# A tile's place in memory, late loads and later transposes in a two-layer decoder trunk

## The chip, the cores and the metric

The kernel runs on one core of a Trainium2 chip. The metric is the device time of one execution in microseconds (us). Three runs of the kernel before took 938.87, 939.19 and 939.3 us; the median is 939.19 us. The engines are named as in the profile: PE multiplies matrices (PEld is its loading of the stationary operand), DVE and ACT work on tiles element by element, POOL does small things and issues some DMAs, SP issues the other DMAs.

## The reference

A trunk of two layers on x of 256 x 1024 in float32. Every layer is FFN, attention, FFN. The first attention is stick-breaking, the second a sliding window with sinks that reads keys and values (kv_w) computed from the stream after layer one.

```
def rms_norm(x, g):
    y = xf * lax.rsqrt(jnp.mean(xf * xf, axis=-1, keepdims=True) + RMS_EPS)
    return (y * g)

def swiglu(x, w_in, w_out):
    gate, up = jnp.split(x @ w_in, 2, axis=-1)
    return (jax.nn.silu(gate) * up) @ w_out

for layer in range(DEPTH):                        # DEPTH = 2, D_FF = 2816
    h = h + 0.5 * swiglu(rms_norm(h, ffn1_norm[layer]), ffn1_w_in[layer], ffn1_w_out[layer])
    hn = rms_norm(h, mix_norm[layer])
    if layer < N_A_LAYERS:                        # 16 heads of 64
        qkv = (hn @ sb_w_qkv[layer])
        h = h + stick_breaking_attention(q, k, v) @ sb_w_o[layer]
    else:                                         # 4 kv heads, window 128
        q = rotary(hn @ swa_w_q[j])
        h = h + sliding_window_sink_attention(q, k_shared, v_shared, swa_sinks[j]) @ swa_w_o[j]
    h = h + 0.5 * swiglu(rms_norm(h, ffn2_norm[layer]), ffn2_w_in[layer], ffn2_w_out[layer])
    if layer == N_A_LAYERS - 1:
        kv = rms_norm(h, kv_norm) @ kv_w
        k_shared, v_shared = rotary(k), v
return rms_norm(h, final_norm)
```

## The kernel before, in words

**Products in parts.** Every float32 factor is split in a high part (a cast to float32r) and a low part (the rest). `step` (L226 is the matmul helper `mm` that it calls) makes three matmuls of it: high stationary on high weights, low stationary on high weights, high stationary on low weights. A weight block arrives as `raw`; ACT casts it to `w_hi` (L345) and DVE subtracts to get `w_lo` (L347), in two pieces each. The stationary operand holds 128 rows of the stream, transposed: `xT` after a norm, `aT_h`/`aT_l` after the FFN's gating, `S_h`/`S_l` for sums of quarters of x, `o_h`/`o_l` after an attention, `xkv_h`/`xkv_l` for the shared keys and values. The weight part streams past it, 512 columns at a time. In the queries of the sliding window the weight part is 256 columns wide; in those and the keys of the stick-breaking attention xT moves and the weights are stationary.

**xT** is one tile `[128, 8, 2, 256]` of 16 KB in each partition, which holds both parts. It is requested at the head of the program, ahead of all other tiles, and a tile takes its place in memory when it is requested: in this build byte 8,320 of each partition. Most other tiles (raw, weight parts, aT, S) come from `Slots` and are requested when the first instruction that uses them is written out.

**An FFN** goes over the 2816 columns in six blocks: one plain, one narrow (256 columns), four by Strassen's scheme with seven products of 12 matmuls instead of eight, three of the seven with xT. In each block gate and up are multiplied together (`mul`, L523, or `mul_less`, L652, on DVE), the result m is transposed on PE (`turn`, L532) into the bank `tr` and split into aT_h (ACT) and aT_l (DVE). The output products of a block follow inside the next one. The first FFN's plain block runs while the first weights are still arriving.

**The order.** Every operation is a `Task` with an engine, a duration that the planner assumes, a priority and its dependences. `Plan.order` plays the tasks through and writes them out in the order found. That order is kept on PE, ACT, DVE and POOL (`manual_schedule` names these four). SP is not among them: its DMAs are ordered by the scheduler of the language, from the program as written out. `lat` of a task is the delay that the planner assumes between its end and the start of a task that needs it.

**Norm weights** (`gain`) are loaded by a DMA that spreads 1024 values over 128 partitions, through two slots. The gain of the next norm is requested ahead of the stage at whose end it is used. The sinks and the rotation table `rp` are requested ahead of the first FFN and used in the second half of the program.

Of the kernel before, what the change touches and what calls it, by code (L numbers as in the profile page):

```python
# [17 lines left out]
P = 128  # L18
# [22 lines left out]
BY_DMA = False  # L41
DMA3 = True
FSUMS = 5000.0
WARM = 14
HEAD = 700.0

# [120 lines left out]
def kernel(  # L167
# [34 lines left out]
    RAW, WP, A4 = Slots("raw", RAWS, 8), Slots("w", 2 * PAIRS, 8), Slots("a", 4, 4)  # L202
    STG, S8, G4 = Slots("stg", 6, 3), Slots("s", 2, 8), Slots("g", 2, 4)

    xx = pool.tile([P, KD, 2, S], F32R, name="xT")
    xh, xl = [Buf(lambda i=i: xx[:, :, i]) for i in range(2)]
    hN = fixed([P, NT, D], F32, "hN")
    kT_s, v_s = fixed([P, KVH, S], F32, "kT_s"), fixed([P, NT, KVH * HD], F32, "v_s")
    ps_all = psum.tile([P, 8, 512], F32, name="ps")
# [94 lines left out]
    MWIN = [(consts, f"mw{i}") for i in range(3)] + K0  # L304


    def dma(src, dst, nbytes, w, prio, name=None):
        T("SP", nbytes / (300.0 if prio < -8e5 else PLAIN), lambda: nc.sync.dma_start(out=dst(), in_=src), w=w, prio=prio)

    def gain(vec):  # L310
        g = G4.get([P, D], F32, "gain")
        dma(vec.unsqueeze(0).to_broadcast([P, D]), lambda: g.ap, P * D * 4, B(g), plan.pos + 20000)
        return g


# [153 lines left out]
    def ffn(w_in, w_out, acc, rest, finish, kv=None, blocks=BLOCKS, first=False, ending=False):  # L469
# [50 lines left out]
            T("ACT", act(n), lambda: ACT.activation(out=dst(), in_=src(), func=AF.Silu), r=r + [(consts, "tbl")], w=w)  # L520

        def mul(dst, a_, b_, r, w, n=512):
            T("DVE", dve(n), lambda: DVE.tensor_mul(out=dst(), in0=a_(), in1=b_()), r=r, w=w)  # L523


        def turn(m, t, aT, nk=4):
# [90 lines left out]
        def strassen(n, c, between):  # L617
            a, d, b = ring
            ring[:] = [d, b, a]
            aT = new_a()  # L620
            r11, r12, r22, r21 = [load([(slice(0, 512), col(h, i, c))], 4, 512) for h, i in ((0, 0), (1, 0), (1, 1), (0, 1))]

            def add(dst, src):
                m = 2048 // PIECES
                for i in range(PIECES):
                    sl = slice(m * i, m * i + m)
                    ks = [i] if PIECES == 2 else [0, 1]
                    T("DVE", dve(m), lambda sl=sl: DVE.tensor_add(out=flat(dst)[:, sl], in0=flat(dst)[:, sl], in1=flat(src)[:, sl]),  # L628
                      r=[(src, k) for k in ks], w=[(dst, k) for k in ks], prio=plan.pos - LEAD)
# [12 lines left out]

            def stage(src, name):
                s = STG.get([P, 512], F32, name)
                T("ACT", act(512), lambda: ACT.copy(out=s.ap, in_=src.ap), r=B(src), w=B(s))
                return s

            def plus(s, bank):
                T("DVE", dve(512), lambda: DVE.tensor_add(out=s.ap, in0=s.ap, in1=bank.ap), r=B(bank), w=B(s))

            def mul_less(dst, a_, b_, r, w):
                T("DVE", dve(512), lambda: DVE.scalar_tensor_tensor(out=dst(), in0=b_(), scalar=-1.0, in1=a_(), op0=ALU.mult, op1=ALU.mult),  # L652
                  r=r, w=w)
# [38 lines left out]
            STG.put(p5)  # L692
            turn(m, 1, aT)
            return aT, 4
# [77 lines left out]
    def stick_breaking(w_qkv, w_o, p0, others_, finish):  # L772
# [85 lines left out]
        for t in range(NT):  # L858
            for j in range(2):
                values(j, t)  # L860
        for g in range(4):
            ws = [weight([(slice(0, 256), wv[:, :, s * D + 256 * g:s * D + 256 * g + 256])], KD, 256) for s in range(2)]

            for b in range(2):
                for s in range(2):
                    ps = bank_()
                    for k in range(KD):
                        hi, lo = ws[s]

                        def run(k=k, hi=hi, lo=lo, ps=ps, b=b):  # L870
                            mm(ps.ap, hi.ap[:, k, ts(b)], xx[:, k].rearrange("p a b -> p (a b)"), k == 0, False)
# [33 lines left out]
    def shared_kv(gk, pairs, rstds):  # L905
        kh, kl = WP.get([P, KD, S], F32R, "xkv_h"), WP.get([P, KD, S], F32R, "xkv_l")

        def operands(tr):
            for t in range(NT):
                normed(t, rstds[t], gk, [tr, tr], kh, kl)  # L910

        def run(ring, tr):
            at_ = plan.pos
            plan.pos -= 8000.0
            operands(tr)
            plan.pos = at_
            wv = by_k(kv_w)
            bs = [ring[0], ring[1]]
# [23 lines left out]
    def sliding_window(w_q, w_o, p0, others_, finish):  # L942
# [165 lines left out]
    A4.put(grow)  # L1108

    def finisher(scale, gs, then=None):  # L1110
        g = gain(gs)

        def fin(t, pair):
            add_residual(t, pair, scale)
            normed(t, None, g, pair, xh, xl)
            if t == 1:
                G4.put(g)
        return fin

    rstds = {}  # L1120
# [10 lines left out]
            normed(t, rstds[t], g0, ring_pair((A0, A1)[t]), xh, xl, (j,))  # L1131
    plan.pos = 0.0
    T("POOL", 10, lambda: None, w=B(g0, banks[6], banks[7]))
    for dst, src, n in ((sinks, swa_sinks[0].unsqueeze(0).to_broadcast([P, H]), P * H * 4),
                        (rp, rope.rearrange("(t p) c d -> p t c d", p=P), P * NT * 4 * HD * 4)):
        dma(src, lambda dst=dst: dst.ap, n, B(dst), 40000)
    T("DVE", 150, lambda: DVE.tensor_scalar(out=nsinks.ap, in0=sinks.ap, scalar1=-1.0, scalar2=None, op0=ALU.mult),
      r=B(sinks), w=B(nsinks), prio=60000)

    ffn(ffn1_w_in[0], ffn1_w_out[0], (A0, A1), A2 + A3, finisher(0.5, mix_norm[0]), first=True)  # L1140
    stick_breaking(sb_w_qkv[0], sb_w_o[0], A0, (A1, A2, A3), finisher(1.0, ffn2_norm[0]))
    ffn(ffn2_w_in[0], ffn2_w_out[0], (A0, A1), A2 + A3, finisher(0.5, ffn1_norm[1]))
    gk = gain(kv_norm)
    ffn(ffn1_w_in[1], ffn1_w_out[1], (A0, A1), A2 + A3, finisher(0.5, mix_norm[1]), kv=shared_kv(gk, (A0, A1), rstds))
    sliding_window(swa_w_q[0], swa_w_o[0], A0, (A2, A3, A1), finisher(1.0, ffn2_norm[1]))

    g_fin = gain(final_norm)

    def last(t, pair):
        add_residual(t, pair, 0.5)  # L1150
        hg = [STG.get([P, 512], F32, "hg") for _ in range(2)]
        rstd = root(t)
        for j in range(2):
            T("DVE", dve(512), lambda j=j: DVE.tensor_mul(out=hg[j].ap, in0=hN.ap[:, t, half(j)], in1=g_fin.ap[:, half(j)]),
              r=[(hN, (t, j))] + B(g_fin), w=B(hg[j]), prio=plan.pos + 10)
# [51 lines left out]
```

## Time and profile before

| | |
|---|---|
| median of 3 runs | 939.19 us |
| the profiled execution | 940.11 us, its span 938.3 us |
| PE busy | 926.3 us (99%) |
| DVE busy | 780.7 us (83%) |
| ACT busy | 602.4 us (64%) |
| read from memory | 204.22 MB, 219 GB/s over the span |
| mean granted TensorE clock | 0.997 |

The span runs from the first to the last instruction. A row of a group shows the line, engine and operation, the tiles written and read, the shape and count, then the busy time of the group in us and the mean duration of one in ns, then the idle time of the engine ahead of it. Matmuls follow each other before the one ahead has ended, and their ends are modelled; the distance from start to start is what one costs in a row of them. In a timeline the first number is the start, the second the time that the merged instructions cover.

### The profile page before, as it was taken

The page shows a single profiled execution, that of the slowest core. Times are in us where ns is not written, and L with a number is a line of the kernel's source. Part 1 is how long each engine was busy: PE and PEld are TensorE (multiplying, and loading weights), DVE is VectorE, ACT ScalarE, POOL GpSimd, SP SyncE. Part 2 cuts the span into 40 slices and gives each one's busy share as a digit, 9 for nine tenths or more (in the row PEclk, how much of TensorE's full clock was granted, in tenths as well). Part 3 has the DMA queues.
Part 4 walks back from the last instruction along what each step waited for, and adds up shares of the span by engine and source line. Part 5 has one row for each costly group of instructions (what it writes and reads, how often), then busy time and mean ns, then how long its engine had stood idle before and what let it go on. Part 6 is the DMA issues. An engine that isn't in the chain of part 4 may idle for free.

```text
span 938.3 us, 11890 instructions
## 1 busy us (share of the span) xinstructions
PE 926.3 (99%) x4520; PEld 754.1 (80%) x4520; DVE 780.7 (83%) x929; ACT 602.4 (64%) x851; POOL 51.7 (6%) x62
## 2 busy tenths in 40 slices
PE   9999999999999999999999999999999999999997
PEld 6788888888887888888888888888887788888885
DVE  7879998766666987999879689998798598799983
ACT  6566767556777656766656467676756475676662
POOL 1010101000000000110000001010000000011000
PEclk9999999999999999999999999999999999999999
DMA  9968999866334677999975579999752348699961
GB/s 326 356 154 236 292 279 241 280 202 224 100 126 134 202 201 203 227 311 272 287 250 190 179 184 268 300 283 243 247 191 91 90 143 244 195 231 308 275 174 45
DMA packets 100203, 206.04 MB, mean 220 GB/s; under 512 B 3761, under 2 KB 24497, under 8 KB 100146
## 3 DMA queue, kind: packets, MB, share of 16 engines
q1 hardware_dynamic: 83104, 171.46, 52.0%
q0 software_dynamic: 16896, 33.56, 21.4%
q8 instruction: 35, 0.57, 0.2%
q10 hardware_dynamic: 146, 0.27, 0.1%
q14 instruction: 22, 0.18, 0.1%
HBM read 204.22 MB, written 1.05 MB: 219 GB/s over the span
## 4 chain that ended last, share of the span: by engine, by line
PE 89%; DVE 4%; DMA 4%; issue 1%; ACT 1%; SPq 0%; POOL 0%; POOLq 0%; DVEq 0%; ACTq 0%
PE ps L226 85%; DMA raw<-in_ffn_w_in_dram 3%; PE ps L532 2%; DVE w_lo L347 2%; PE ps L396 1%; DMA raw<-in_swa_w_q_dram 1%; ACT w_hi L345 1%; DVE e L1048 0%; DVE xs L450 0%; ACT sq L421 0%; DVE small L1022 0%; DVE xT L403 0%; DVE hN L463 0%; DVE s L498 0%; PE ps L1055 0%
## 5 line engine op out<-in xcount | busy, mean ns | idle before, releaser
L347 DVE TENSOR_TENSOR w_lo<-raw,w_hi 128x1024 fp32r<-128x1024 f32 x412 | 484.7, 1219 | 46.0 <-ACT w_hi L345 44.2
L345 ACT CAST w_hi<-raw 128x1024 fp32r<-128x1024 f32 x412 | 410.6, 1049 | 122.0 <-PE ps L226 58.3
L226 PE MATMUL ps<-w_hi,xT 128*128 128x512 f32 (+1 forms) x960 | 288.8, 384 | 0.9 <-ACT xT L402 0.6
L226 PEld LDWEIGHTS ps<-w_hi,xT 128*128 128x128 f32 x960 | 175.2, 189 | 37.4 <-ACT xT L402 0.9
L226 PE MATMUL ps<-w_lo,xT 128*128 128x512 f32 (+1 forms) x480 | 183.0, 381 | 0.0
L226 PE MATMUL ps<-w_hi,aT_h 128*128 128x512 f32 x352 | 139.3, 396 | 0.0
L226 PE MATMUL ps<-w_lo,aT_h 128*128 128x512 f32 x352 | 137.5, 391 | 0.0
L226 PE MATMUL ps<-w_hi,aT_l 128*128 128x512 f32 x352 | 137.0, 389 | 0.0
L226 PEld LDWEIGHTS ps<-w_lo,xT 128*128 128x128 f32 x480 | 90.6, 189 | 18.9
L226 PE MATMUL ps<-w_hi,S_h 128*128 128x512 f32 x256 | 101.6, 397 | 0.0
L226 PE MATMUL ps<-w_lo,S_h 128*128 128x512 f32 x256 | 100.1, 391 | 0.0
L226 PE MATMUL ps<-w_hi,S_l 128*128 128x512 f32 x256 | 99.7, 389 | 0.0
L226 PEld LDWEIGHTS ps<-w_lo,aT_h 128*128 128x128 f32 x352 | 66.1, 188 | 14.2
L226 PEld LDWEIGHTS ps<-w_hi,aT_l 128*128 128x128 f32 x352 | 66.2, 188 | 13.3
L226 PEld LDWEIGHTS ps<-w_hi,aT_h 128*128 128x128 f32 x352 | 66.1, 188 | 13.0
L628 DVE TENSOR_TENSOR raw<-raw 128x1024 f32<-128x1024 f32 x64 | 76.1, 1219 | 0.4
L633 POOL DMA_DIRECT2D raw<-in_ffn_w_in_dram x32 | 41.0, 1282 | 537.7 <-ACT w_hi L345 224.5
L226 PEld LDWEIGHTS ps<-w_lo,S_h 128*128 128x128 f32 x256 | 48.0, 188 | 10.4
L226 PEld LDWEIGHTS ps<-w_hi,S_l 128*128 128x128 f32 x256 | 48.1, 188 | 9.7
L226 PEld LDWEIGHTS ps<-w_hi,S_h 128*128 128x128 f32 x256 | 48.1, 188 | 9.7
L402 ACT CAST aT_h<-ps 128x512 fp32r<-128x512 f32 (+1 forms) x48 | 26.4, 550 | 35.2 <-PE ps L532 35.1
L226 PE MATMUL ps<-xT,w_hi 128*128 128x512 f32 x128 | 46.5, 401 | 0.0
(154 smaller groups left out, 889.5 us busy)
## 6 DMA issues: line engine op xcount, KB each, us to landing
raw<-in_ffn_w_in_dram SPq DMA_DIRECT2D x76, 1024.0 KB, 7.8
raw<-in_ffn_w_out_dram SPq DMA_DIRECT2D x44, 1024.0 KB, 5.2
raw<-in_ffn_w_in_dram POOLq DMA_DIRECT2D x32, 1024.0 KB, 9.3
raw<-in_sb_w_qkv_dram SPq DMA_DIRECT2D x12, 1024.0 KB, 6.6
raw<-in_ffn_w_in_dram SPq DMA_DIRECT2D x16, 512.0 KB, 5.0
raw<-in_ffn_w_in_dram SPq DMA_DIRECT2D x16, 256.0 KB, 5.4
raw<-in_sb_w_o_dram SPq DMA_DIRECT2D x4, 1024.0 KB, 5.1
raw<-in_swa_w_q_dram SPq DMA_DIRECT2D x4, 1024.0 KB, 9.4
```

What stands on the lines that cost most here:

```text
L226: PE.matmul(ps, lhsT=lhsT, rhs=rhs, start=start, stop=stop, skip_group_check=True)
L345: T("ACT", act(m), lambda sl=sl: ACT.copy(out=flat(hi)[:, sl], in_=flat(raw)[:, sl]), r=[(raw, i) for i in rs] + first, w=[(hi, i) for i i ...
L347: T("DVE", dve(m), lambda sl=sl: DVE.tensor_sub(out=flat(lo)[:, sl], in0=flat(raw)[:, sl], in1=flat(hi)[:, sl].bitcast(F32)), r=[(raw, i) ...
L396: PE.transpose(out=bank.ap[:, i * P:(i + 1) * P], in_=s, identity=ident)
L402: T("ACT", act(n), lambda: ACT.copy(out=hi[2](), in_=src()), r=B(bank), w=[hi[0:2]])
L532: PE.transpose(out=tr.ap[:, i * P:(i + 1) * P], in_=m.ap[:, i * P:(i + 1) * P], identity=ident)
L628: T("DVE", dve(m), lambda sl=sl: DVE.tensor_add(out=flat(dst)[:, sl], in0=flat(dst)[:, sl], in1=flat(src)[:, sl]), r=[(src, k) for k in ks ...
L633: T("POOL", 1500, lambda: nc.gpsimd.dma_start(out=dst.ap, in_=src, accum_op=ALU.add), w=[(dst, 0), (dst, 1)], prio=plan.pos - LOADS, lat=5 ...
```

## The change

Four edits, as the diff below shows them:

- xT is requested when the first instruction that writes it is written out, behind the first raw tiles and weight parts. In the build its place goes from byte 8,320 to byte 85,600 of each partition. The tiles that lay between the two, two of the weight slots, two of the raw slots and one of the two aT_l slots among them, move down by 16,384 bytes; the rest stay, but for a swap of an aT_h and a gain slot.
- Each gain is requested at the end of its stage, with a dependence on a marked late tile of that stage and an earlier priority than the point of request; the sinks and `rp` are requested behind the stick-breaking attention, with a dependence of the same kind. The dependence is the planner's; no data goes over it.
- `mul` and `mul_less` get a `lat` of 1180 instead of 180: the planner counts with 1000 ns more until the transposes of their result may run.
- `nsinks`, one small DVE operation on the sinks, moves with them.

```
+TM = 1000.0
...
-    xx = pool.tile([P, KD, 2, S], F32R, name="xT")
-    xh, xl = [Buf(lambda i=i: xx[:, :, i]) for i in range(2)]
+    xT = Buf(lambda: pool.tile([P, KD, 2, S], F32R, name="xT"))
+    xh, xl = [Buf(lambda i=i: xT.ap[:, :, i]) for i in range(2)]
...
-    def dma(src, dst, nbytes, w, prio, name=None):
+    def dma(src, dst, nbytes, w, prio, r=()):
...
+    marks = []
     def gain(vec):
         g = G4.get([P, D], F32, "gain")
-        dma(vec.unsqueeze(0).to_broadcast([P, D]), lambda: g.ap, P * D * 4, B(g), plan.pos + 20000)
+        dma(vec.unsqueeze(0).to_broadcast([P, D]), lambda: g.ap, P * D * 4, B(g), plan.pos - 25000, marks)
...
-            T("DVE", dve(n), lambda: DVE.tensor_mul(out=dst(), in0=a_(), in1=b_()), r=r, w=w)
+            T("DVE", dve(n), lambda: DVE.tensor_mul(out=dst(), in0=a_(), in1=b_()), r=r, w=w, lat=LAT["DVE"] + TM)
...
-                  r=r, w=w)
+                  r=r, w=w, lat=LAT["DVE"] + TM)
...
+            if n == last - 1:
+                marks[:] = [(outs[n][0][0], 1)]
...
+        marks[:] = [(v, (0, 1))]
...
+        marks[:] = [(qT, (2, 1))]
...
     def finisher(scale, gs, then=None):
-        g = gain(gs)
+        g = []
         def fin(t, pair):
+            if t == 0:
+                g.append(gain(gs))
             add_residual(t, pair, scale)
-            normed(t, None, g, pair, xh, xl)
+            normed(t, None, g[0], pair, xh, xl)
...
-        dma(src, lambda dst=dst: dst.ap, n, B(dst), 40000)
+        dma(src, lambda dst=dst: dst.ap, n, B(dst), plan.pos - 60000, marks)
```

What becomes of it in the order of the instructions is shown at three places. The first is PE's queue where the first FFN's plain block ends (its last products with xT) and the transposes of its first m stand. Before:

```order
L226 MATMUL ps<-w_hi,xT 128x512 x2
L226 MATMUL ps<-w_lo,xT 128x512
L532 MATMUL ps<-ident,m 128x128 [waits DVE_49]
L532 MATMUL ps<-ident,m 128x128 x3
L226 MATMUL ps<-w_hi,xT 128x512 [waits Activation_49]
L226 MATMUL ps<-w_hi,xT 128x512
L226 MATMUL ps<-w_lo,xT 128x512
```

And in the change:

```order
L228 MATMUL ps<-w_hi,xT 128x512 x2
L228 MATMUL ps<-w_lo,xT 128x512
L228 MATMUL ps<-w_hi,xT 128x512 [waits Activation_49]
L228 MATMUL ps<-w_hi,xT 128x512
L228 MATMUL ps<-w_lo,xT 128x512 [waits DVE_49]
L537 MATMUL ps<-ident,m 128x128 [waits DVE_49]
L537 MATMUL ps<-ident,m 128x128 x3
```

One step of the narrow block, three matmuls, now stands ahead of the transposes; the same happens at the other transposes of the FFNs.

The second is SP's queue in the first FFN, from the narrow block's weights on. Before:

```order
L308 DMA raw<-in_ffn_w_in_dram 128x4x256 x4
L308 DMA gain<-in_mix_norm_dram 128x1024
L308 DMA sinks<-in_swa_sinks_dram 128x16
L308 DMA rp<-in_rope_dram 128x2x256
L308 DMA gain<-in_ffn_norm_dram 128x1024
L308 DMA raw<-in_ffn_w_out_dram 128x2x1024 x2
```

And in the change:

```order
L310 DMA raw<-in_ffn_w_in_dram 128x4x256 x4
L310 DMA gain<-in_mix_norm_dram 128x1024
L310 DMA sinks<-in_swa_sinks_dram 128x16
L310 DMA rp<-in_rope_dram 128x2x256
L310 DMA gain<-in_ffn_norm_dram 128x1024
L310 DMA raw<-in_ffn_w_out_dram 128x2x1024 x2
```

Nothing moved there; the whole of SP's queue has the same loads in the same order in both builds.

The third is DVE's queue in a Strassen block of the first FFN, around the split of a transposed m (aT_l). Before:

```order
L347 TENSOR_TENSOR w_lo<-raw,w_hi 128x1024 x2
L652 SCALAR_TENSOR_TENSOR m<-p_818,m 128x512
L347 TENSOR_TENSOR w_lo<-raw,w_hi 128x1024 x2
L403 TENSOR_TENSOR aT_l<-ps,aT_h 128x4x128
L347 TENSOR_TENSOR w_lo<-raw,w_hi 128x1024 x6
```

And in the change:

```order
L352 TENSOR_TENSOR w_lo<-raw,w_hi 128x1024 x2
L657 SCALAR_TENSOR_TENSOR m<-p_807,m 128x512
L352 TENSOR_TENSOR w_lo<-raw,w_hi 128x1024 x3
L408 TENSOR_TENSOR aT_l<-ps,aT_h 128x4x128
L352 TENSOR_TENSOR w_lo<-raw,w_hi 128x1024 x5
```

The split of the transposed m moved behind one more piece of a weight.

More of the change, by code (lines that the diff above doesn't have):

```diff
@@ L304 @@
     MWIN = [(consts, f"mw{i}") for i in range(3)] + K0
-    def dma(src, dst, nbytes, w, prio, name=None):
-        T("SP", nbytes / (300.0 if prio < -8e5 else PLAIN), lambda: nc.sync.dma_start(out=dst(), in_=src), w=w, prio=prio)
+    def dma(src, dst, nbytes, w, prio, r=()):
+        T("SP", nbytes / (300.0 if prio < -8e5 else PLAIN), lambda: nc.sync.dma_start(out=dst(), in_=src), r=r, w=w, prio=prio)
+    marks = []
     def gain(vec):
         g = G4.get([P, D], F32, "gain")
-        dma(vec.unsqueeze(0).to_broadcast([P, D]), lambda: g.ap, P * D * 4, B(g), plan.pos + 20000)
+        dma(vec.unsqueeze(0).to_broadcast([P, D]), lambda: g.ap, P * D * 4, B(g), plan.pos - 25000, marks)
         return g
@@ L870, in run @@
                         def run(k=k, hi=hi, lo=lo, ps=ps, b=b):
-                            mm(ps.ap, hi.ap[:, k, ts(b)], xx[:, k].rearrange("p a b -> p (a b)"), k == 0, False)
+                            mm(ps.ap, hi.ap[:, k, ts(b)], xT.ap[:, k].rearrange("p a b -> p (a b)"), k == 0, False)
                             mm(ps.ap[:, 0:S], lo.ap[:, k, ts(b)], xh.ap[:, k], False, k == KD - 1)
@@ L903, in rotary, with shared_kv, operands @@
         T("DVE", dve(2 * n), lambda: DVE.tensor_add(out=dst(), in0=dst(), in1=tmp.ap), r=[(tmp, 0), (tmp, 1)], w=w)
-    def shared_kv(gk, pairs, rstds):
+    def shared_kv(vec, pairs, rstds):
         kh, kl = WP.get([P, KD, S], F32R, "xkv_h"), WP.get([P, KD, S], F32R, "xkv_l")
-        def operands(tr):
+        def operands(tr, gk):
             for t in range(NT):
@@ L914, in run @@
             plan.pos -= 8000.0
-            operands(tr)
+            gk = gain(vec)
+            operands(tr, gk)
             plan.pos = at_
@@ L1110, in finisher @@
     def finisher(scale, gs, then=None):
-        g = gain(gs)
+        g = []
         def fin(t, pair):
+            if t == 0:
+                g.append(gain(gs))
             add_residual(t, pair, scale)
-            normed(t, None, g, pair, xh, xl)
+            normed(t, None, g[0], pair, xh, xl)
             if t == 1:
-                G4.put(g)
+                G4.put(g[0])
         return fin
@@ L1133 @@
     T("POOL", 10, lambda: None, w=B(g0, banks[6], banks[7]))
+    ffn(ffn1_w_in[0], ffn1_w_out[0], (A0, A1), A2 + A3, finisher(0.5, mix_norm[0]), first=True)
+    stick_breaking(sb_w_qkv[0], sb_w_o[0], A0, (A1, A2, A3), finisher(1.0, ffn2_norm[0]))
     for dst, src, n in ((sinks, swa_sinks[0].unsqueeze(0).to_broadcast([P, H]), P * H * 4),
                         (rp, rope.rearrange("(t p) c d -> p t c d", p=P), P * NT * 4 * HD * 4)):
-        dma(src, lambda dst=dst: dst.ap, n, B(dst), 40000)
+        dma(src, lambda dst=dst: dst.ap, n, B(dst), plan.pos - 60000, marks)
     T("DVE", 150, lambda: DVE.tensor_scalar(out=nsinks.ap, in0=sinks.ap, scalar1=-1.0, scalar2=None, op0=ALU.mult),
-      r=B(sinks), w=B(nsinks), prio=60000)
-    ffn(ffn1_w_in[0], ffn1_w_out[0], (A0, A1), A2 + A3, finisher(0.5, mix_norm[0]), first=True)
-    stick_breaking(sb_w_qkv[0], sb_w_o[0], A0, (A1, A2, A3), finisher(1.0, ffn2_norm[0]))
+      r=B(sinks), w=B(nsinks), prio=plan.pos)
     ffn(ffn2_w_in[0], ffn2_w_out[0], (A0, A1), A2 + A3, finisher(0.5, ffn1_norm[1]))
-    gk = gain(kv_norm)
-    ffn(ffn1_w_in[1], ffn1_w_out[1], (A0, A1), A2 + A3, finisher(0.5, mix_norm[1]), kv=shared_kv(gk, (A0, A1), rstds))
+    ffn(ffn1_w_in[1], ffn1_w_out[1], (A0, A1), A2 + A3, finisher(0.5, mix_norm[1]), kv=shared_kv(kv_norm, (A0, A1), rstds))
     sliding_window(swa_w_q[0], swa_w_o[0], A0, (A2, A3, A1), finisher(1.0, ffn2_norm[1]))
-    g_fin = gain(final_norm)
+    g_fin = []
     def last(t, pair):
+        if t == 0:
+            g_fin.append(gain(final_norm))
         add_residual(t, pair, 0.5)
@@ L1153, in last @@
         for j in range(2):
-            T("DVE", dve(512), lambda j=j: DVE.tensor_mul(out=hg[j].ap, in0=hN.ap[:, t, half(j)], in1=g_fin.ap[:, half(j)]),
-              r=[(hN, (t, j))] + B(g_fin), w=B(hg[j]), prio=plan.pos + 10)
+            T("DVE", dve(512), lambda j=j: DVE.tensor_mul(out=hg[j].ap, in0=hN.ap[:, t, half(j)], in1=g_fin[0].ap[:, half(j)]),
+              r=[(hN, (t, j))] + B(g_fin[0]), w=B(hg[j]), prio=plan.pos + 10)
         for j in range(2):
```

## The prediction, made before the changed kernel was run

> **What bounds the kernel now.** I read the busy shares first, then the chain of work that ended last, then TensorE's groups with shapes kept apart, then its timeline.
>
> ```profile
> span 938.3 us, 11890 instructions
> PE 926.3 (99%) x4520; PEld 754.1 (80%) x4520; DVE 780.7 (83%) x929; ACT 602.4 (64%) x851; POOL 51.7 (6%) x62
> PE 89%; DVE 4%; DMA 4%; issue 1%; ACT 1%; SPq 0%; POOL 0%; POOLq 0%; DVEq 0%; ACTq 0%
> ```
>
> TensorE (PE) is busy for 926.3 of 938.3 us and carries 89% of the chain. Some 12 us of idle time are all that removing waits could win; beyond that the matmuls themselves must follow each other faster. So I asked whether they all cost the same.
>
> ```profile
> L226 PE MATMUL ps<-w_hi,xT 128*128 128x512 f32 x832 | 264.5, 399 | 0.8 <-ACT xT L402 0.6 <-DVE xT L403 0.2
> L226 PE MATMUL ps<-w_lo,xT 128*128 128x512 f32 x416 | 165.0, 397 | 0.0
> L226 PE MATMUL ps<-w_lo,aT_h 128*128 128x512 f32 x352 | 137.5, 391 | 0.0
> L226 PE MATMUL ps<-w_hi,aT_l 128*128 128x512 f32 x352 | 137.0, 389 | 0.0
> L226 PE MATMUL ps<-w_hi,S_l 128*128 128x512 f32 x256 | 99.7, 389 | 0.0
> L226 PE MATMUL ps<-w_hi,xkv_l 128*128 128x512 f32 x16 | 6.2, 389 | 0.0
> ```
>
> All are 512 columns wide, with a weight part moving and the second-named tile stationary. With xT stationary one takes 397 to 399 ns, with aT, S and xkv mostly 389 to 391. Their ends are modelled, so the pace must come from starts:
>
> ```profile
> 20.13 0.63 PE L226 MATMUL ps<-w_hi,xT 128*128 128x512 f32 x2
> 34.13 0.63 PE L226 MATMUL ps<-w_hi,xT 128*128 128x512 f32 x2
> 917.87 13.64 PE ps L226 x60
> 667.04 0.39 PE L226 MATMUL ps<-w_hi,aT_h 128*128 128x512 f32 x1
> 671.80 0.39 PE L226 MATMUL ps<-w_hi,aT_h 128*128 128x512 f32 x1
> 538.86 0.39 PE L226 MATMUL ps<-w_hi,xkv_h 128*128 128x512 f32 x1
> 540.90 0.39 PE L226 MATMUL ps<-w_hi,xkv_h 128*128 128x512 f32 x1
> ```
>
> Between the two xT rows lie 20 steps of three matmuls: 14.00 us / 60 = **233.3 ns**. Between the two aT rows lie 21: 4.76 / 21 = 226.7 ns; the chain's 60 at the end (aT alone) give 13.64 / 60 = **227.3 ns**. Between the xkv rows lie nine: 2.04 / 9 = 226.7 ns. The same helper at L226, with the same weight slots moving, is 6.0 ns slower per matmul when xT is the stationary operand.
>
> **The operand's tile.** xT is the only stationary operand of this kind at the bottom of a partition (byte 8,320 in the build); the change puts it at 85,600. xkv_l lies at byte 85,600 already, and its rows above run at 226.7 ns. So at the new place I take 227.3. The saving is 233.3 - 227.3 = 6.0 ns each. Of 832 + 416 = 1,248 such matmuls the first FFN block holds 96 (32 steps of three); they are over before the wait for data at 36.86 us treated below, so what they save only lengthens that wait. That leaves 1,152 x 6.0 ns = **6.9 us**. Bounds: a run of xkv rows that holds slower starts (537.47 to 540.90 us, 15 matmuls) gives 228.7 ns, so 4.6 ns and 5.3 us; 226.7 gives 6.6 ns and 7.6 us.
>
> ```profile
> 537.47 0.40 PE L226 MATMUL ps<-w_hi,xkv_h 128*128 128x512 f32 x1
> L226 PE MATMUL ps<-w_lo,xT 128*128 128x256 f32 x64 | 18.0, 281 | 0.0
> L226 PE MATMUL ps<-xT,w_lo 128*128 128x256 f32 x128 | 36.0, 281 | 0.0
> ```
>
> The 192 matmuls of 256 columns with xT stationary get nothing: they take the same 281 ns as those of that width with a weight stationary.
>
> The cover for the 6.9 us is DVE's and the DMA's slack, since the weights must now come as fast:
>
> ```profile
> 80.00:180.00 100.00, 100.00 (x454) 82.12 (x452) 93.77 (x94) 67.96 (x80) 7.64 (x6) 1.00 0.97 276
> 770.00:790.00 20.00, 20.00 (x91) 16.15 (x90) 19.93 (x21) 12.44 (x16) 1.30 (x1) 1.00 0.70 224
> PEld ps L226 <- DVE w_lo L347: 1.0, 4, 0.2
> ```
>
> The columns are the stretch, its length, then busy PE, PEld, DVE, ACT, POOL. A Strassen block is 84 matmuls of products, 36 of them with xT, and 48 of output: 36 x 6.0 = 0.22 us of about 30, or 0.7%. DVE goes from 93.8 to 94.4% there and the DMA from 0.97 to 0.98; both still fit. From 770 to 790 us, at the last FFN's first block, DVE is busy for 19.93 of 20.00 us while PE runs on xT nearly alone and would want to be 0.5 us shorter. DVE splits weights ahead of use (weight loads waited 1.0 us for w_lo in the whole run), so I give back between 0 and 0.5 us, taken as **0.2**.
>
> **The transposes, one product later.** What this can win is PE's wait for the product m:
>
> ```profile
> 34.60 0.40 PE L226 MATMUL ps<-w_lo,xT 128*128 128x512 f32 x1
> 33.86 2.35 DVE L347 TENSOR_TENSOR w_lo<-raw,w_hi 128x1024 fp32r<-128x1024 f32 x2
> 36.13 0.68 DVE L523 TENSOR_TENSOR m<-m,ps 128x512 f32<-128x512 f32 x1
> 36.86 0.66 PE L532 MATMUL ps<-ident,m 128*128 128x128 f32 x4 [1.86 <-DVE m L523]
> PE ps L532 <- DVE m L523: 1.9, 1, 1.9
> ```
>
> The waits' table has one such wait, 1.9 us, in the whole run: after the first block, PE stands before the transposes (L532) while DVE finishes two w_lo pieces and then the multiplication. In the changed order one step of the next block (three matmuls) stands ahead of them. Its third matmul needs the first of the two pieces, which ends near 33.86 + 1.2 = 35.1 us, so the step is done by about 35.6, inside the wait. The transposes still start at 36.86, since DVE's own order up to m is unchanged, and PE has one step less to do afterwards: 0.70 us (14.00 / 20). Gain **0.7 us**. At the other turns PE waited for nothing, so the shift wins 0. What is late next is aT_h and aT_l, by a step and in places by one more w_lo in DVE's queue (1.2 us, half of the two above); their output matmuls come at least a dozen matmuls later, so 0 there too.
>
> The wait has a second price, the clock:
>
> ```profile
> 34.62:38.04 3.42, 1.55 (x9) 1.07 (x8) 3.42 (x5) 3.42 (x4) 0.00 (x0) 1.00 0.81 266
> 38.04:41.45 3.41, 3.41 (x9) 2.63 (x8) 3.41 (x5) 2.51 (x4) 0.00 (x0) 0.50 1.05 393
> 41.45:44.86 3.41, 3.41 (x18) 2.80 (x17) 3.41 (x4) 0.59 (x1) 0.00 (x0) 1.00 1.03 323
> ```
>
> After a stretch in which PE was busy for 1.55 of 3.42 us the granted clock was 0.50 for 3.41 us: 9 matmuls there and 18 in the next stretch, so about 1.7 us lost. One step more in the gap makes that stretch some 0.5 us busier; whether this keeps the clock no row tells. I count 0 and keep 1.7 for the low end. The Trainium skill (TensorE: Matmul & The Clock Gate, Why this matters for your kernels) warns of idle gaps above about 3 us only. By that rule the gap here would not lower the clock and shortening it wins nothing more; the trace disagrees, since a gap of 1.86 us was followed by the half clock.
>
> **Late loads: nothing.** The edit wants two gains, the sinks and the rotation table out of the start.
>
> ```profile
> gain<-in_ffn_norm_dram SPq DMA_DIRECT2D x3, 512.0 KB, 5.6
> rp<-in_rope_dram SPq DMA_DIRECT2D x1, 256.0 KB, 7.5
> ...
> 16.30 1.87 SPq L308 DMA_DIRECT2D gain<-in_mix_norm_dram  x1
> 19.52 0.56 SPq L308 DMA_DIRECT2D gain<-in_ffn_norm_dram  x1
> 20.19 1.98 SPq L308 DMA_DIRECT2D raw<-in_ffn_w_out_dram  x2
> ACT w_hi L345 <- DMA raw<-in_ffn_w_out_dram: 3.5, 1, 3.5
> ```
>
> They do stand ahead of the w_out load for which ACT then waited 3.5 us, and moving 1.25 MB (512 + 256 + 512 KB, the gain of mix_norm being as large) behind it would be worth about that wait. But SP is not among the engines whose order the planner writes, and in the changed build its queue has the same loads in the same order. Gain 0; if they did move, 3.5 us at most, less what the transposes took of the same wait. The nsinks multiplication on DVE does move, one instruction of 16 elements: 0.
>
> **Sum.** 6.9 + 0.7 - 0.2 = 7.4 us. The profiled execution took 940.11 us (span 938.3 and 1.8 around it), so 932.7 for its like; the median of the runs, 939.19, stands 0.9 lower, so **931.8 us**. Own range: the best of all bounds, 7.6 + 0.7 + 1.7 = 10.0, gives 929.2; the worst, 5.3 + 0.4 - 0.5 = 5.2 (0.4 for a startup step that partly waits), gives 934.0.
>
> **Rivals.** *A. The place is not the cause.* The 6 ns belong to the way xT is used or filled, and stay. Then only the startup remains: 939.19 - 0.7 = 938.5. For it: xT differs from the others in more than its place; it alone holds both halves, hi and lo, in one tile of 16 KB, and the change leaves that. Against it: xkv is made and used as xT is, through the same lines, and is fast. The Trainium skill (SBUF — State Buffer, SBUF: two separate sides) says that PE and ACT "never wait on anyone" at their ports and names no cost of where in a partition an operand starts; by that rule this rival is right. The trace speaks against it with 233.3 beside 227.3 ns. Chance 0.13.
>
> *B. Low places are slow, and another tile moves into one.* With xT gone from the bottom, everything below its new place moves down 16,384 bytes; half of the aT_l tiles go from byte 46,688, where they are fast, to 30,304. xT fills bytes 8,320 to 24,703, so the border of the slow part is unknown between the two. Each aT_l matmul stands between two with aT_h. If 30,304 is slow, 352 / 2 = 176 of them pay 6.0 ns, 1.1 us, and if the matmul that each hands over to pays as well, 2.1 us: up to 931.8 + 2.1 = 933.9. Chance 0.12.
>
> *C. Slower: the new place is dearer.* xT now lies among the slots that are being filled and streamed, and a stationary read there might be held up more than at the bottom. If the surcharge doubles to 12 ns, 1,152 x 6.0 = 6.9 us are added and 0.7 won: 945.4. It decides from 0.7 us / 1,152 = 0.6 ns over today's 233.3 ns; from 2.3 ns on it shows as slower. Against it: xkv's 226.7 ns at that very byte. Chance 0.06.
>
> **How the numbers follow.** The forecast has 0.69 (its clock and slack variants included), B 0.12, A 0.13, C 0.06. Forecast and B together hold 0.81, so the range is 929.2 to 935.5 (B with the forecast's lower gains). About 0.2% (1.9 us) can be told from no change: the forecast and B are faster, 0.81; A is the same, 0.13; C is slower, 0.06.
>
> **What would show it.** Right: xT groups of 512 columns at 389 to 391 ns, an xT step of three in 0.68 us, PE's busy sum some 7 us lower. The wait before the first transposes is split, about 1.2 us of it right before them. SP's first rows are the same. B would show as aT_l rows above 391 ns; A as xT still at 395 or more; C as over 400. The forecast is wrong if DVE's splits become PE's releasers in Strassen blocks, or if the first L532 wait stays at 1.9 us.

## The result, and the profile after

The changed kernel took 932.88 us (median of 6 runs, 931.37 to 933.38) where the kernel before, run beside it, took 939.23 us (6 runs, 938.81 to 941.39). The ratio is 0.9928, with a 95% interval of 0.9915 to 0.994. So 6.35 us were won; 7.4 had been predicted.

The first rows of the profiled page after, in the order in which they were read before: the span, the busy shares, the shares of the chain of work that ended last.

```profile
span 931.6 us, 11900 instructions
PE 920.4 (99%) x4520; PEld 755.6 (81%) x4520; DVE 779.6 (84%) x929; ACT 602.0 (65%) x851; POOL 51.8 (6%) x62
PE 92%; DVE 4%; DMA 2%; SPq 1%; issue 0%; ACT 0%; POOL 0%; POOLq 0%; DVEq 0%; ACTq 0%
```

The span is 6.7 us shorter (this execution took 933.38 us) and PE's busy time 5.9 us less (926.3 to 920.4). The idle time is as it was, some 11 to 12 us. So nearly all of the gain is matmuls that follow each other faster. PE's groups after, the shapes kept apart:

```profile
L228 PE MATMUL ps<-w_hi,xT 128*128 128x512 f32 x832 | 259.6, 393 | 0.0
L228 PE MATMUL ps<-w_lo,xT 128*128 128x512 f32 x416 | 163.0, 392 | 0.6 <-DVE w_lo L352 0.6
L228 PE MATMUL ps<-w_hi,aT_l 128*128 128x512 f32 x352 | 137.0, 389 | 0.0
L228 PE MATMUL ps<-xT,w_hi 128*128 128x512 f32 x128 | 47.1, 407 | 0.0
L228 PE MATMUL ps<-w_hi,xT 128*128 128x256 f32 x128 | 24.5, 290 | 0.1
```

The two xT groups fell from 264.5 + 165.0 to 259.6 + 163.0 us: 6.9 us. The aT_l group, half of whose tiles moved to byte 30,304, is as it was at 389 ns. The last two rows went the other way. These are the groups of the kernel before in which xT takes part without being the stationary operand of 512 columns:

```profile
L226 PE MATMUL ps<-xT,w_hi 128*128 128x512 f32 x128 | 46.5, 401 | 0.0
L226 PE MATMUL ps<-w_hi,xT 128*128 128x256 f32 x128 | 24.3, 288 | 0.0
```

In the keys of the first attention xT moves and the weight is stationary; that group now costs 0.6 us more. PE's timeline after, at the first plain block and its end:

```profile
19.87 0.62 PE L228 MATMUL ps<-w_hi,xT 128*128 128x512 f32 x2
33.47 0.62 PE L228 MATMUL ps<-w_hi,xT 128*128 128x512 f32 x2
34.83 0.61 PE L228 MATMUL ps<-w_hi,xT 128*128 128x512 f32 x2
36.09 0.50 PE L228 MATMUL ps<-w_lo,xT 128*128 128x512 f32 x1 [0.64 <-DVE w_lo L352]
37.82 0.66 PE L537 MATMUL ps<-ident,m 128*128 128x128 f32 x4 [1.23 <-DVE m L528]
```

Twenty steps take 13.60 us: 226.7 ns for each matmul, where before it was 233.3. Then one step stands ahead of the transposes as planned, and the wait is split, 0.64 + 1.23 = 1.87 us, as long in all as the 1.86 us before. But the transposes start at 37.82, not at 36.86. The same place in the granted clock (stretch, length, then PE, PEld, DVE, ACT, POOL, then the clock, the DMA's share and GB/s), and the last FFN's first block:

```profile
35.13:38.54 3.41, 1.54 (x8) 0.87 (x7) 3.41 (x4) 3.41 (x5) 0.00 (x0) 1.00 0.75 204
38.54:41.96 3.42, 3.42 (x10) 2.67 (x9) 3.42 (x5) 2.97 (x4) 0.00 (x0) 0.50 1.05 399
765.00:785.00 20.00, 20.00 (x95) 16.58 (x94) 20.00 (x21) 12.45 (x18) 1.30 (x1) 1.00 0.73 223
```

The stretch at half the clock came again. In the last FFN's first block DVE has nothing left (20.00 of 20.00 us), and PE is not idle for it. Last, SP's queue after:

```profile
16.44 1.93 SPq L310 DMA_DIRECT2D gain<-in_mix_norm_dram  x1
18.42 0.78 SPq L310 DMA_DIRECT2D sinks<-in_swa_sinks_dram  x1
19.24 0.43 SPq L310 DMA_DIRECT2D rp<-in_rope_dram  x1
19.72 0.56 SPq L310 DMA_DIRECT2D gain<-in_ffn_norm_dram  x1
20.39 2.58 SPq L310 DMA_DIRECT2D raw<-in_ffn_w_out_dram  x2
```

The "late" loads stand where they stood, ahead of w_out. The pair of w_out issues ends at 20.39 + 2.58 = 22.97 us, 0.8 us later than before (20.19 + 1.98 = 22.17), and ACT starts on what was loaded 0.96 us later. Its row after, and its row before:

```profile
31.45 7.69 ACT L350 CAST w_hi<-raw 128x1024 fp32r<-128x1024 f32 x8 [3.87 <-DMA raw<-in_ffn_w_out_dram]
```

```profile
30.49 7.69 ACT L345 CAST w_hi<-raw 128x1024 fp32r<-128x1024 f32 x8 [3.52 <-DMA raw<-in_ffn_w_out_dram]
```

DVE's w_lo pieces and m follow behind these casts: 31.45 - 30.49 = 0.96 us later, and the transposes with them. This delay is not shown to be the work of the change: m starts at 36.13 us in the one trace of the kernel before, and between 36.8 and 37.6 us in all the traces below that keep SP's queue as it was, with the later transposes and without them.

### The profile page after: what moved, and what is told of

Read it like the earlier page. It is cut to its first block, busy times and chain, and to the rows that moved or that the text cites. A ratio compares the mean times of both kernels' runs of the same rounds, so it can differ in the third digit from the quotient of the medians.

```text
span 931.6 us, 11900 instructions
## 1 busy us (share of the span) xinstructions
PE 920.4 (99%) x4520; PEld 755.6 (81%) x4520; DVE 779.6 (84%) x929; ACT 602.0 (65%) x851; POOL 51.8 (6%) x62
## 4 chain that ended last, share of the span: by engine, by line
PE 92%; DVE 4%; DMA 2%; SPq 1%; issue 0%; ACT 0%; POOL 0%; POOLq 0%; DVEq 0%; ACTq 0%
PE ps L228 88%; PE ps L537 2%; DVE w_lo L352 2%; DMA raw<-in_ffn_w_in_dram 1%; DMA raw<-in_ffn_w_out_dram 1%; PE ps L401 1%; SPq L310 1%; DVE e L1057 0%; DVE xs L455 0%; DVE small L1031 0%; DVE xT L408 0%; PE ps L1064 0%; DVE hN L468 0%; DVE o_l L408 0%; POOL small L433 0%
## 5 line engine op out<-in xcount | busy, mean ns | idle before, releaser
L228 PE MATMUL ps<-w_hi,xT 128*128 128x512 f32 (+1 forms) x960 | 284.1, 379 | 0.1
L228 PE MATMUL ps<-w_lo,xT 128*128 128x512 f32 (+1 forms) x480 | 181.0, 377 | 0.6 <-DVE w_lo L352 0.6
```

Of the source, the lines that this page charges most:

```text
L228: PE.matmul(ps, lhsT=lhsT, rhs=rhs, start=start, stop=stop, skip_group_check=True)
```

## The experiments

Nine kernels were run, each beside the kernel before. The theory to be tested was that of the prediction: the 6 ns belong to xT's place at the bottom of a partition. All times are medians.

### 1. One part alone: move_only and rest_only

move_only is the kernel before with only xT requested late; rest_only is the changed kernel with xT requested at the head of the program again.

```
move_only, against the kernel before
-    xx = pool.tile([P, KD, 2, S], F32R, name="xT")
-    xh, xl = [Buf(lambda i=i: xx[:, :, i]) for i in range(2)]
+    xT = Buf(lambda: pool.tile([P, KD, 2, S], F32R, name="xT"))
+    xh, xl = [Buf(lambda i=i: xT.ap[:, :, i]) for i in range(2)]

rest_only, against the changed kernel
-    xT = Buf(lambda: pool.tile([P, KD, 2, S], F32R, name="xT"))
+    xT = fixed([P, KD, 2, S], F32R, "xT")
```

> The kernel before with xT alone requested late (byte 85,600 instead of 8,320); loads and transposes as before. Theory (the place costs 6 ns per matmul with xT stationary): xT groups of 512 columns at 389 to 393 ns instead of 397 to 399, the wait of 1.9 us before the first transposes stays or grows by about 0.5 us, time 932.0 to 933.0 us. Rival (most of the gain came with the new order of the transposes): 938 us or more.

> The changed kernel with xT back at byte 8,320; late requests of the loads and later transposes stay. Theory: xT groups back at 397 to 399 ns, the first wait before the transposes 0.7 us shorter, time 938.0 to 939.0 us, not to be told from the kernel before. Rival: 933 us.

move_only took 934.13 us against 939.41 (ratio 0.9936, 0.9919 to 0.9954), so 5.3 us less. rest_only took 938.35 (0.9987, 0.9977 to 0.9996), 1.1 us less. Together that is 6.3 us, as much as the whole gain. move_only won 1.1 us less than the least that was expected of it; the expectation had no term for the losses in the other matmuls with xT, which are counted further below. The xT group in move_only, and then in rest_only:

```profile
L226 PE MATMUL ps<-w_hi,xT 128*128 128x512 f32 x832 | 258.4, 392 | 0.0
L226 PE MATMUL ps<-xT,w_hi 128*128 128x512 f32 x128 | 47.1, 407 | 0.0
```

```profile
L228 PE MATMUL ps<-w_hi,xT 128*128 128x512 f32 x832 | 263.1, 397 | 0.0
L228 PE MATMUL ps<-xT,w_hi 128*128 128x512 f32 x128 | 46.5, 401 | 0.0
```

Both the gain and the small loss in the keys go with xT's place and with nothing else. But these two don't tell what about the place counts.

### 2. What about the place? Shifts by 32 bytes

The build gives a detail that the prediction did not use. All tile starts are multiples of 32 bytes. Before, xT at byte 8,320 starts at 128 modulo 256 (the rest of 8,320 when divided by 256), and the weight parts, aT_l and xkv all at 96 (77,408, 46,688, 85,600). After, xT at 85,600 starts at 96 as well. So there is a second theory: not where xT lies counts, but how its start stands to that of the weight part that moves past it. Since all slices that the matmuls take start at multiples of 512 bytes within their tiles, the tiles' starts decide. Fillers of a few bytes, written once and used by nothing else, move tiles and change little else.

low_plus32 leaves xT at the bottom and shifts it by 32 bytes, with a second filler behind it, so that it agrees with the rest. high_plus32 leaves xT at its high place and shifts it by 32 bytes, so that it does not.

```
low_plus32, against the kernel before
+    pads = [pool.tile([P, 8], F32, name="pad0")]
     xx = pool.tile([P, KD, 2, S], F32R, name="xT")
+    pads.append(pool.tile([P, 8], F32, name="pad1"))
...
+    T("DVE", 120, lambda: [DVE.memset(p, 0.0) for p in pads], prio=9e5)

high_plus32, against the changed kernel
-    xT = Buf(lambda: pool.tile([P, KD, 2, S], F32R, name="xT"))
+    def make_xT():
+        pads = [pool.tile([P, 8], F32, name="pad0")]
+        t = pool.tile([P, KD, 2, S], F32R, name="xT")
+        pads.append(pool.tile([P, 8], F32, name="pad1"))
...
+    xT = Buf(make_xT)
```

> The kernel before with xT 32 bytes higher, at 8,352, which like every weight part is an odd multiple of 32; two fillers of 32 bytes keep all other tiles on odd multiples. Two theories of why the old place was dear. Low part of the partition: xT groups stay at 397 to 399 ns, time 938.5 to 939.5 us. Alignment (xT stood on an even multiple of 32, all other operands on odd ones): xT groups fall to 389 to 393 ns, time 932 to 933 us.

> The changed kernel with xT 32 bytes higher, at 85,632, an even multiple of 32; all other tiles on odd multiples as they were. Low part of the partition: xT groups stay at 392 to 393 ns, time 932 to 933.5 us. Alignment: xT groups rise to 397 to 399 ns, time 938 to 939 us.

low_plus32 took 935.63 us (ratio 0.9953, 0.9933 to 0.9974): most of the gain, with xT still at the bottom. high_plus32 took 942.79 us (1.0032, 1.0021 to 1.0042): slower than the kernel before, with xT high. The first and the last of an unbroken row of xT steps in PE's timeline of low_plus32, and then of high_plus32:

```profile
19.31 0.62 PE L228 MATMUL ps<-w_hi,xT 128*128 128x512 f32 x2
33.59 0.62 PE L228 MATMUL ps<-w_hi,xT 128*128 128x512 f32 x2
```

```profile
19.16 0.63 PE L235 MATMUL ps<-w_hi,xT 128*128 128x512 f32 x2
33.86 0.63 PE L235 MATMUL ps<-w_hi,xT 128*128 128x512 f32 x2
```

Twenty-one steps of three lie between the rows of each pair: 14.28 us / 63 = 226.7 ns at the bottom, 14.70 / 63 = 233.3 ns high up. low_plus32 stayed 2.8 us above the changed kernel. It lacks the later transposes, and in its trace PE is done with the first block earlier and waits longer for m; its table of waits has

```profile
PE ps L535 <- DVE m L526: 3.3, 1, 3.3
```

where the kernel before has 1.9 us. How the 2.8 us divide was not measured. **The prediction's reason, the bottom of the partition, falls here.** high_plus32 became slower than the kernel before because the fillers also set aT and weight slots apart: two weight slots and one aT_l slot stay at 96 modulo 256 and the tiles behind xT go to 160, and with that S and aT pay too. Summed from start to start behind 45 us, the matmuls of 512 columns with a weight moving and another tile than xT stationary take 480.6 us there and 477.0 us in the kernel before. These are two groups of aT, in which only some of the matmuls pay:

```profile
L235 PE MATMUL ps<-w_hi,aT_l 128*128 128x512 f32 x352 | 138.0, 392 | 0.0
L235 PE MATMUL ps<-w_lo,aT_h 128*128 128x512 f32 x352 | 138.0, 392 | 0.0
```

### 3. Relative or absolute, and with which period

Two readings were left: certain starts are slow by themselves (128 modulo 256, say), or the distance between the two operands counts. others_plus32 leaves xT at byte 8,320 and puts one filler of 32 bytes behind it, so that all the other large tiles go from 96 to 128 modulo 256 and agree with xT. low_plus96 shifts xT by 96 bytes and the others by 256: the two then agree modulo 128 but stand 128 apart modulo 256. others_plus288 is others_plus32 with a filler of 288 bytes: agreement modulo 256, 256 apart modulo 512.

```
others_plus32, against the kernel before
     xx = pool.tile([P, KD, 2, S], F32R, name="xT")
+    pads.append(pool.tile([P, 8], F32, name="pad1"))

others_plus288, against the kernel before
     xx = pool.tile([P, KD, 2, S], F32R, name="xT")
+    pads.append(pool.tile([P, 72], F32, name="pad1"))

low_plus96, against the kernel before
+    pads.append(pool.tile([P, 24], F32, name="pad0"))
     xx = pool.tile([P, KD, 2, S], F32R, name="xT")
+    pads.append(pool.tile([P, 40], F32, name="pad1"))
```

> The kernel before; xT stays at byte 8,320 (a multiple of 128), and one filler of 32 bytes behind it moves every other large tile from 96 to 0 behind a multiple of 128. Phase theory (a matmul is fast when its stationary and its moving operand start at the same distance behind a multiple of 128 bytes): all groups at 389 to 393 ns though xT has not moved, time 933 to 935 us. Theory that a start on an even multiple of 32 bytes is slow by itself: all groups at 395 to 399 ns, some 1,800 further matmuls slower by 6 ns, time 948 to 952 us.

> The kernel before with xT 96 bytes higher (8,416) and fillers of 256 bytes in all, so that xT agrees with the weight parts modulo 128 but stands 128 apart from them modulo 256. Phase with a period of 128 bytes or less: xT groups at 389 to 393 ns, time 933 to 936 us. Period of 256 or more: 395 to 399 ns, time 938.5 to 940 us.

> The kernel before, with xT at byte 8,320 as ever and 288 bytes of filler behind it, so that all the other large tiles start 288 bytes higher. Modulo 512, xT then starts at 128 and the weight parts at 384: they agree modulo 256 and stand 256 apart modulo 512. If what counts is whether the stationary and the moving operand start at the same byte modulo 256, the xT matmuls start every 227 ns, their groups show 390 to 392 ns, and the time is 932.9 to 936.6 us, as with 32 bytes of filler. If the period is 512 bytes or more, they start every 233 ns, the groups show 396 to 398 ns, and the time stays at 939 to 941 us, as in the kernel before.

others_plus32 took 934.02 us against 939.7 (ratio 0.9934, 0.9917 to 0.995), low_plus96 939.96 (1.0002, 0.9991 to 1.0012), others_plus288 935.16 against 939.87 (0.995, 0.9933 to 0.9966). The rows of steps, in this order:

```profile
19.24 0.62 PE L228 MATMUL ps<-w_hi,xT 128*128 128x512 f32 x2
34.20 0.62 PE L228 MATMUL ps<-w_hi,xT 128*128 128x512 f32 x2
```

```profile
19.47 0.62 PE L229 MATMUL ps<-w_hi,xT 128*128 128x512 f32 x2
34.11 0.62 PE L229 MATMUL ps<-w_hi,xT 128*128 128x512 f32 x2
```

```profile
19.14 0.61 PE L228 MATMUL ps<-w_hi,xT 128*128 128x512 f32 x2
34.10 0.61 PE L228 MATMUL ps<-w_hi,xT 128*128 128x512 f32 x2
```

Twenty-two steps in 14.96 us are 226.7 ns, twenty-one in 14.64 us are 232.4 ns, twenty-two in 14.96 us are 226.7 ns. In others_plus32 xT did not move by a byte and became fast, so the distance counts. All seven cases, with the start modulo 256:

| kernel | xT at byte | xT, modulo 256 | weight parts, modulo 256 | ns per matmul | time, us |
|---|---|---|---|---|---|
| before | 8,320 | 128 | 96 | 233.3 | 939.2 |
| after | 85,600 | 96 | 96 | 226.7 | 932.9 |
| low_plus32 | 8,352 | 160 | 160 | 226.7 | 935.6 |
| others_plus32 | 8,320 | 128 | 128 | 226.7 | 934.0 |
| others_plus288 | 8,320 | 128 | 128 (256 apart modulo 512) | 226.7 | 935.2 |
| low_plus96 | 8,416 | 224 | 96 | 232.4 | 940.0 |
| high_plus32 | 85,632 | 128 | 160, two slots 96 | 233.3 | 942.8 |

The kernels before that ran beside them took 939.2 to 939.9 us. Distances of 32 and 128 bytes modulo 256 cost 6 ns, a distance of 256 costs nothing. high_plus32 has one more distance, in one and the same execution: by the slots that the build gives to each matmul, those with S or aT stationary start every 227 ns (median, behind 45 us) where both operands agree, and every 231 to 234 ns where they stand 64 bytes apart, in either direction. So the period is 256 among the distances that were tried; 96 was not. What in the chip does this stays open; the runs show the rule, not its cause.

### 4. Loads that really move: sp_planned

The late loads of the changed kernel did not move, because SP's order is not the planner's. sp_planned makes it so.

```
-    ctx.enter_context(tc.manual_schedule(engines={getattr(mybir.EngineType, e) for e in ("PE", "Activation", "DVE", "Pool")}))
+    ctx.enter_context(tc.manual_schedule(engines={getattr(mybir.EngineType, e) for e in ("PE", "Activation", "DVE", "Pool", "SP")}))
```

> The changed kernel with SP's queue, too, written in the planner's order, so that the gains, the sinks and the rotation table do load late and a w_out load goes ahead of half of the narrow block's weights. If the loads held up the start: the wait before the first transposes goes, up to 3.5 us less than the changed kernel, 929.5 to 932 us. Rival (the planner's order makes SP wait at the head of its queue for slots that come free late, behind which other loads stand): 934 us or more.

It took 929.87 us against 939.7 (4 runs, 929.15 to 931.0; ratio 0.9894, 0.988 to 0.9909), the fastest of all: some 3 us below the changed kernel. SP's queue, and then PE at the first transposes:

```profile
18.72 0.37 SPq L310 DMA_DIRECT2D raw<-in_ffn_w_out_dram  x1
21.55 0.37 SPq L310 DMA_DIRECT2D raw<-in_ffn_w_out_dram  x1
...
155.88 1.08 SPq L310 DMA_DIRECT2D gain<-in_mix_norm_dram  x1
```

```profile
36.10 0.60 PE L537 MATMUL ps<-ident,m 128*128 128x128 f32 x4
36.46 0.71 PE L228 MATMUL ps<-w_hi,xT 128*128 128x512 f32 x2
```

The first w_out load is issued ahead of everything that is not needed yet, the gain at 155.88 us. The transposes start at 36.10 us without any wait, 1.7 us earlier than in the changed kernel, and no stretch at half the clock follows. The two together make the gain: compared matmul by matmul, this trace leads that of the changed kernel by 1.7 us at the transposes, by 3.4 us at 43 us and by 3.3 us at the end.

### 5. The wait and the clock: bridged

To see whether PE's gap brings the half clock, bridged fills it: ten small bf16 matmuls ahead of the first transposes, into the bank that the transposes then overwrite. Nothing uses what they compute.

```
+            fill = 10 if first and bridged.append(m) is None and len(bridged) == 1 else 0
...
             def run():
+                for _ in range(fill):
+                    mm(tr.ap[:, 0:S], warm.to_broadcast([P, P]), warm.to_broadcast([P, S]), True, True)
```

> The changed kernel with ten matmuls of no use, 256 columns in bf16, between the step of the narrow block and the first transposes, where PE waits some 1.2 us. If the wait brings on the half clock: no stretch at 0.50 between 34 and 45 us, and a median 0.7 to 1.7 us below the changed kernel, 931.2 to 932.2. Rival (the half clock there does not hang on this wait): the time as the changed kernel's, 932.9 us, or 1 us more if the ten run past the wait.

It took 932.32 us (4 runs, 931.58 to 932.55; ratio 0.9918, 0.9903 to 0.9933). The stretches of its clock around the gap:

```profile
36.58:39.99 3.41, 3.41 (x23) 2.77 (x22) 3.41 (x5) 3.41 (x5) 0.00 (x0) 1.00 0.97 360
39.99:43.40 3.41, 3.41 (x18) 2.83 (x17) 3.41 (x6) 2.12 (x3) 0.00 (x0) 1.00 1.05 392
```

The clock stays at 1.00. But this trace is no clean test: m is done at 37.73 us and the ten matmuls keep PE until 38.41, so that the wait which they filled was under 0.5 us and they ran past it; and in rest_only, which has no bridge, the transposes follow at 37.55 us without a wait and the clock stays at 1.00 as well. In time this is 0.6 us less than the changed kernel, and the two intervals overlap, so the bridge alone is inconclusive: three of the six runs of the changed kernel had a granted clock of 0.998 without a bridge and took 931.37 to 932.68 us, the three at 0.995 took 933.08 to 933.38. More is told by the traces of the kernels that were run for other reasons. Each shows the clock changing only at the borders of stretches of 3.41 us, and the borders lie elsewhere in each execution. The stretch that held the wait for m, in others_plus32 and in others_plus288, with the one behind it:

```profile
35.84:39.26 3.42, 1.83 (x11) 1.29 (x10) 3.42 (x5) 3.42 (x5) 0.00 (x0) 1.00 0.84 276
39.26:42.67 3.41, 3.34 (x18) 2.50 (x17) 3.41 (x5) 2.94 (x5) 0.00 (x0) 1.00 1.03 386
```

```profile
34.25:37.67 3.42, 1.38 (x7) 0.80 (x5) 3.42 (x4) 3.42 (x5) 0.00 (x0) 1.00 0.43 87
37.67:41.08 3.41, 2.80 (x9) 2.42 (x10) 3.41 (x5) 3.41 (x6) 0.00 (x0) 0.50 1.04 402
```

With 1.83 of 3.42 us busy the clock stayed; with 1.38 it was halved for the next stretch. Before it was 1.55 and halved, after 1.54 and halved, in move_only 1.94 and not halved. The traces hold more such stretches, at 855 us in others_plus32 and at the ends of the runs. In all eleven traces, from 13 us on, a stretch at full clock in which PE was busy for 1.55 us or less was followed by half the clock, and one with 1.56 us or more was not. PE's ends are modelled, so the last digit is not to be relied on; the border lies near 46% of a stretch. In the first 13 us this does not hold: in the changed kernel a stretch with 3.06 us busy (4.41 to 7.82 us) was followed by half the clock, in the kernel before one with 2.79 us (7.32 to 10.73 us) was not. PE's work there is warm-up matmuls, a product of one row and transposes. So busy time alone is not what decides, and what does stays open.

## Why the prediction was right, and where it was wrong

The time fell as forecast, 932.88 us for 931.8, and the edit that was to bring it did. By its own steps:

- **The operand's tile, 6.9 us.** The step that failed is its reason: "xT is the only stationary operand of this kind at the bottom of a partition". The bottom has nothing to do with it (low_plus32 and others_plus32 are fast there, high_plus32 slow high up). What changed is the distance of xT's start from that of the weight parts, modulo 256 bytes. The number held all the same, because the row that carried it, xkv at byte 85,600, agrees with the weights in the same way as xT does there; by the reason alone a place 32 bytes higher would have done as well, and it does not (high_plus32), so that the reason led to a fast place was luck. As a size it was somewhat too large. Summed from start to start behind 45 us, 1,127 stationary xT matmuls take 264.0 us before and 1,128 take 257.8 us after: 234.2 and 228.5 ns, so 5.7 ns each and 6.4 us. And matmuls for which the prediction had "nothing" or no term lost: the 128 with xT moving over 512 columns went from a median of 228 to 236 ns (30.7 to 31.4 us in sum), the 192 of 256 columns with xT stationary from 118 to 120 ns (24.2 to 24.5 us). Net that is 6.4 - 0.7 - 0.3 = 5.4 us, and move_only measured 5.3. The groups with xT stationary show 393 and 392 ns, not the 389 to 391 that were named as the sign.
- **The transposes, 0.7 us.** rest_only measured 1.1 us (0.4 to 2.2 by its interval), but does not show it to be this step's: in its trace PE's first block ends some 2 us later than before, the transposes follow at 37.55 us without any wait, and no stretch at half the clock comes. In the profile after, the step stands ahead of the transposes, as forecast; that they start at 36.86 us was the wrong half of it. DVE's order up to m was the same, but m came 0.96 us later, behind the later w_out loads, so in this execution the step won nothing at the first transposes. Why SP issued the second of these loads 0.8 us later stays open.
- **The give-back of 0.2 us to DVE** did not show: DVE is full from 765 to 785 us and PE does not wait there. What was given back was given back in the keys' matmuls.
- **The clock, counted 0.** The stretch came again in the profiled execution, since its busy part (1.54 us) was not raised by the extra step; with the later m the step only filled what the delay had added. Whether it comes in the run that gave the median no trace shows. The Trainium skill (TensorE: Matmul & The Clock Gate, What's actually happening) describes a free-running window of 3413 ns; the stretches of 3.41 us here agree. From 13 us on, the busy share of one such window told in these traces whether the next one was halved. The advice of the Trainium skill (TensorE: Matmul & The Clock Gate, Why this matters for your kernels) to avoid gaps of over some 3 us is too lenient by these traces: the 1.86 us of the kernel before were enough. A wait of 1.85 us that ends at 857.62 us in others_plus32 was not, with 1.56 us busy in its window against 1.55.
- **Late loads, 0.** Right: the rows of SP's queue are the same. The bound, "3.5 us at most, less what the transposes took of the same wait", came near: sp_planned won 3 us when they moved, but about half of that, in the traces, is the half clock that stayed away, which the bound did not hold.
- **Rival A** (the place is not the cause) falls by move_only. **Rival B** (low places are slow, aT_l at 30,304 pays) falls by aT_l's 389 ns. **Rival C** (the new place is dearer) falls at byte 85,600. In high_plus32, 32 bytes further, xT costs the old 233.3 ns again and not more; that this kernel took 942.8 us comes from S and aT.
- **The range.** Its upper end, 935.5 us, does not follow from the prediction's own numbers: 934.0 and B's 1.1 to 2.1 us make 935.1 to 936.1.

## What to carry to other kernels

When matmuls with one operand run some per cent slower than their like, compare where the tiles of both operands start, modulo 256 bytes: a filler of 32 bytes behind the operand's tile (others_plus32) won 5.7 us here, nearly as much as the whole change. A row of the profile that runs fast under the conditions that one wants is a safer ground for a number than a theory of why the other row is slow. And an order that a planner works out holds only on the queues that are given to it; look at the queue itself for whether a moved load has moved.

## What was not expected of the hardware

- A matmul of 512 columns in float32r with a stationary operand of 128 x 128 starts every 226.7 ns in a row of them if both operands start at the same byte modulo 256, and every 232.4 to 233.3 ns if they stand 32 or 128 bytes apart (231 to 234 ns at 64 bytes, as a median within high_plus32).
- With the roles exchanged the order of the cases is another. In the keys of the first attention, where 512 columns of xT move past w_hi and 256 past w_lo in turn, agreement is the slower case: a median of 236 ns for the 512 columns in every kernel in which they agree, 228 before (32 bytes apart), 233 in low_plus96 (128 apart). The three pairs from the first to the last of these rows, before, take 1.04 us, and after, 1.06:

```profile
217.43 0.39 PE L226 MATMUL ps<-xT,w_hi 128*128 128x512 f32 x1
218.47 0.39 PE L226 MATMUL ps<-xT,w_hi 128*128 128x512 f32 x1
```

```profile
215.61 0.40 PE L228 MATMUL ps<-xT,w_hi 128*128 128x512 f32 x1
216.67 0.40 PE L228 MATMUL ps<-xT,w_hi 128*128 128x512 f32 x1
```

Why is open; so the rule above is one for streams of full width with the weight moving, as far as these runs go.

- From 13 us on, half the clock came behind a window of 3.41 us in which PE was busy for 1.55 us or less, wherever its borders happened to lie, and not behind one with 1.56 us or more. So a wait of 1.86 us brought it in one trace, and one of 1.85 us in another did not. The stretch at half the clock costs some 1.7 us, an estimate from the 9 matmuls in it before and the 18 in the next one. In the first 13 us the rule fails.
